# Moving the state-space constants of a two-block transformer kernel from VectorE to GpSimd

## The chip, the cores and the metric

The kernel runs on one core of a Trainium2 chip. A core has five engines that each work through a queue of their own, in order: TensorE (PE, matmuls; its weight loads are shown as PEld), VectorE (DVE), ScalarE (ACT), GpSimd (POOL) and SyncE (SP, which here issues the loads of the weights). An instruction waits at the head of its queue until the semaphores of its inputs allow it, and everything behind it on that engine waits too. The metric is device time in microseconds (us) for one execution, lower is better.

## The reference

The reference is a stack of two models on 256 tokens of width 1024. Only the first layer of the first model matters here. It projects the normalised input to a mix of an RWKV-7 recurrence (4 pairs of heads here) and a diagonal state-space model, S5, with 32 groups of 64 complex states. What the S5 part computes from its parameters, before any token is touched, is:

```
lam     = complex(lam_re, lam_im)
dt      = exp(log_dt)[:, None]
lam_bar = exp(lam * dt)
b_bar   = ((lam_bar - 1.0) / lam)[..., None] * complex(b_re, b_im)
bu      = einsum('gpi,btgi->btgp', b_bar, ug)
states  = scan(x_t = lam_bar * x_(t-1) + bu_t)
y       = real(einsum('gip,btgp->btgi', complex(c_re, c_im), states)) + d_skip * ug
```

followed by a gelu and a gate. The 32 x 64 states are laid out as 128 partitions x 16 columns, so that each step on the constants is one operation on a 128x16 tile.

## The kernel before, in words

The kernel goes through ten phases. The first, mix0, holds what the change touches. It normalises the input and transposes it (norm_T, L385 transposes, L361 xTh on ScalarE, L362 xTl on VectorE), and then projects it with weights that are split into a high and a low part: raw is loaded by SyncE into three buffers, ScalarE rounds it (L270, whi), VectorE subtracts (L271, wlo, 128x1024), and TensorE does three matmuls for each product (L320 to L322). The projections come in pairs of blocks (zpair), in the order WA, G0, k0, r0, v0, k1, ... Each block is scaled and token-shifted (L1060 to L1062, zs and z).

Between the normalisation and the RWKV code stands s5_prep, the function that is changed. It loads three tiles (s5l, s5b, s5c) from ScalarE's queue; computes two exponentials by range reduction and a polynomial of degree eight (exp_parts, names dt... and rho...); reduces the angle to (-pi, pi); has ScalarE take one Sine of 128x48 (L1388, tile sn, with a table load); renormalises the cosine and sine (unit, tiles m1 and m2); forms the factor wr + i wi of the B weights with one reciprocal (L1416); multiplies the B weights with it in six GpSimd operations of 128x512 (L1425 to L1427, tiles e2 and bt, shown as e and bt); lets TensorE transpose e2 (L1434) and ScalarE copy the result to WB (L1435); and last squares the cosine and sine seven times for the powers 2, 4, ..., 128 of the rotation (tiles qc and qs). All operations on 128x16 tiles but the Sine are VectorE's, most of them through the helper tt, whose line is L1359.

Who uses the results: WB and rho go into s5_main, whose first matmuls (L1480) come after all projections; the powers go into s5_table (L1453 to L1462), in which GpSimd doubles a table of cosines and sines seven times, from 128x16 to 128x1024. That table lies in memory that the transposed input xTh and xTl held, so it starts after the last projection's matmul.

GpSimd has other short work in the same stretch, in ew, once for each pair of heads: th (L1133), which VectorE's scan L1144 reads, and a (L1139); and zG (L1082). Each is a 128x256 operation between two of other engines.

The order of each engine's queue is not written out by hand in this stage. The kernel is built with a scheduler of the library (TileContext with schedule_with_timeline_sim=True), which plays the program against its own costs of the instructions and puts each instruction into its engine's queue in the order of that play; on the chip the queues keep that order. Semaphores are placed for each dependence, within an engine too. The functions of RWKV are generators that are stepped in turns (drive), which sets the order in which the scheduler meets them.

Of the kernel before, what the change touches and what calls it, by code (L numbers as in the profile page):

```python
# [204 lines left out]
def build(tc, dram, off, out, phases):  # L205
# [10 lines left out]
    V, S, G, T = nc.vector, nc.scalar, nc.gpsimd, nc.tensor  # L216
# [9 lines left out]
    def psC(shape=(128, 512)):  # L226
        return pp.tile(list(shape), F32, tag="C", name="psC", bufs=2)
# [747 lines left out]
    def mix0():  # L975
        nonlocal junk_at
        with tc.tile_pool(name="z", bufs=1, reuse_waits="tile") as zp:
# [16 lines left out]
            with tc.tile_pool(name="rw", bufs=1, reuse_waits="tile") as rp:  # L994
                open_kv(0)
                zx, s5x = ExitStack(), ExitStack()
                zxp = zx.enter_context(tc.tile_pool(name="zx", bufs=1, side="right", reuse_waits="tile"))
                junk_at = (zxp, 512)
                xh, xl, rm = norm_T(ht, "norm_mix0", xp=zxp)
                bcast_row(rm, zp, rrow)  # L1000
                with tc.tile_pool(name="s5prep", bufs=1, reuse_waits="tile") as sp:
                    s5c = s5_prep(zp, sp)

                def s5():
                    zx.close()
                    sp = s5x.enter_context(tc.tile_pool(name="s5", bufs=1, side="right", reuse_waits="tile"))
                    yield from s5_table(sp, s5c)
                    yield from s5_main(sp, s5c, yab, uT)

                rwkv(rp, zpair, yab, uT, rrow, s5())  # L1010
                s5x.close()
# [316 lines left out]
    def gb(x, n=32):  # L1328
        return x[:, :, None].to_broadcast([128, 16, n])

    def s5_prep(zp, sp):
        def t16(name, n=1):
            keep = name in ("rho", "sn") or name[0] == "q"
            return (zp if keep else sp).tile([128, n * 16], F32, name=name)

        lv = sp.tile([128, 48], F32, name="s5l")
        S.dma_start(lv, dram("s5l"))
        bb = sp.tile([128, 2, 512], F32, name="s5b")
        S.dma_start(bb.rearrange("p a b -> p (a b)"), dram("s5b"))
        cc = zp.tile([128, 2, 16, 32], F32, name="s5c")  # L1340
        S.dma_start(cc.rearrange("p a b c -> p (a b c)"), dram("s5c"))
        S.mul(cc[:, 1], cc[:, 1], -1.0)
        lr, li, ld = lv[:, :16], lv[:, 16:32], lv[:, 32:]

        def exp_parts(x, tag):
            n, r, q, s = [sp.tile([128, 16], F32, name=tag + c) for c in "nrqs"]
            V.tensor_scalar(x, x, -87.0, 87.0, op0=ALU.max, op1=ALU.min)
            V.tensor_scalar(n, x, 1.0 / math.log(2.0), 12582912.0, op0=ALU.mult, op1=ALU.add)
            V.tensor_scalar(n, n, -12582912.0, None, op0=ALU.add)
            V.scalar_tensor_tensor(r, n, -0.693359375, x, op0=ALU.mult, op1=ALU.add)  # L1350
            V.scalar_tensor_tensor(r, n, 2.12194440e-4, r, op0=ALU.mult, op1=ALU.add)
            V.tensor_scalar(q, r, 1.0 / 40320, None, op0=ALU.mult)
            for f in (5040, 720, 120, 24, 6, 2, 1):
                V.scalar_tensor_tensor(q, q, 1.0 / f, r, op0=ALU.add, op1=ALU.mult)
            V.tensor_scalar(s.bitcast(I32), n, 127.0, 8388608.0, op0=ALU.add, op1=ALU.mult)
            return q, s

        def tt(o, a, b, op):
            V.tensor_tensor(o, a, b, op=op)  # L1359
            return o  # L1360

        q, s = exp_parts(ld, "dt")
        dt = t16("dt")
        V.scalar_tensor_tensor(dt, q, 1.0, s, op0=ALU.add, op1=ALU.mult)
        ar, th = t16("ar"), t16("theta")
        tt(ar, lr, dt, ALU.mult)
        tt(th, li, dt, ALU.mult)
        q, s = exp_parts(ar, "rho")
        rho, rm1 = t16("rho"), t16("rm1")
        V.scalar_tensor_tensor(rho, q, 1.0, s, op0=ALU.add, op1=ALU.mult)  # L1370
        tt(rm1, q, s, ALU.mult)
        V.scalar_tensor_tensor(rm1, s, -1.0, rm1, op0=ALU.add, op1=ALU.add)
        n, an = t16("turns"), t16("ang", 3)
        r = an[:, :16]
        V.tensor_scalar(n, th, 1.0 / (2 * math.pi), 12582912.0, op0=ALU.mult, op1=ALU.add)
        V.tensor_scalar(n, n, -12582912.0, None, op0=ALU.add)
        c1 = 6.28125
        c2 = 2029.0 / 2 ** 20
        c3 = 2 * math.pi - c1 - c2
        V.scalar_tensor_tensor(r, n, -c1, th, op0=ALU.mult, op1=ALU.add)  # L1380
        V.scalar_tensor_tensor(r, n, -c2, r, op0=ALU.mult, op1=ALU.add)
        V.scalar_tensor_tensor(r, n, -c3, r, op0=ALU.mult, op1=ALU.add)
        V.tensor_scalar(r, r, 3.1415925, -3.1415925, op0=ALU.min, op1=ALU.max)
        V.scalar_tensor_tensor(an[:, 16:32], r, -1.0, r, op0=ALU.mult, op1=ALU.max)
        V.tensor_scalar(an[:, 16:32], an[:, 16:32], -1.0, math.pi / 2, op0=ALU.mult, op1=ALU.add)
        V.tensor_scalar(an[:, 32:], r, 0.5, None, op0=ALU.mult)
        sn = t16("sn", 3)
        S.activation(sn, an, AF.Sin)  # L1388
        m1, m2 = t16("m1"), t16("m2")

        def unit(c, s):
            tt(m1, c, c, ALU.mult)
            tt(m2, s, s, ALU.mult)
            tt(m1, m1, m2, ALU.add)
            V.tensor_scalar(m1, m1, -0.5, 1.5, op0=ALU.mult, op1=ALU.add)
            tt(c, c, m1, ALU.mult)
            tt(s, s, m1, ALU.mult)

        si, co, hs = sn[:, :16], sn[:, 16:32], sn[:, 32:]
        unit(co, si)  # L1400
        br, bi, w1, w2 = t16("br"), t16("bi"), t16("w1"), t16("w2")
        tt(hs, hs, hs, ALU.mult)
        tt(br, rm1, co, ALU.mult)
        V.scalar_tensor_tensor(br, hs, -2.0, br, op0=ALU.mult, op1=ALU.add)
        tt(bi, rho, si, ALU.mult)
        wr, wi = t16("wr"), t16("wi")
        tt(w1, br, lr, ALU.mult)
        tt(w2, bi, li, ALU.mult)
        tt(wr, w1, w2, ALU.add)
        tt(w1, bi, lr, ALU.mult)  # L1410
        tt(w2, br, li, ALU.mult)
        tt(wi, w1, w2, ALU.subtract)
        tt(w1, lr, lr, ALU.mult)
        tt(w2, li, li, ALU.mult)
        tt(w1, w1, w2, ALU.add)
        V.reciprocal(w2, w1)  # L1416
# [12 lines left out]
        for j2 in range(2):  # L1429
            pt = psC((128, 2, 2, 128))  # L1430
            for a in range(2):
                for i in range(2):
                    j = 2 * j2 + a
                    T.transpose(pt[:, a, i], e2[:, i, 4 * j:4 * j + 4].rearrange("p g i -> p (g i)"), ident)  # L1434
            S.copy(WB[:, 2 * j2:2 * j2 + 2], pt)  # L1435

        pw = [(co, si)]
        for i in range(7):
            pc, ps = pw[-1]
            qc, qs = t16("qc%d" % i), t16("qs%d" % i)  # L1440
            tt(m1, pc, pc, ALU.mult)
            tt(m2, ps, ps, ALU.mult)
            tt(qc, m1, m2, ALU.subtract)
            V.scalar_tensor_tensor(qs, pc, 2.0, ps, op0=ALU.mult, op1=ALU.mult)
            unit(qc, qs)
            pw.append((qc, qs))
        return {"pw": pw, "rho": rho, "WB": WB, "cc": cc}
# [384 lines left out]
```

## Time and profile before

| | |
|---|---|
| median of 3 runs | 2523.37 us (2523.07 to 2532.45) |
| the profiled execution | 2523.59 us, of it the span from the first to the last instruction 2521.7 us |
| instructions | 39316; PE 14335, DVE 3506, ACT 2268, POOL 145 |
| mean granted TensorE clock | 0.971 of full speed (2.4 GHz) |

The profile divides the span into stretches; the first phase, mix0, takes about the first 340 us of it. In a timeline each row has the start, the duration (or the sum of those of merged instructions), the engine, the line and the operation, what it writes and reads with the shapes, and in brackets how long the engine stood idle just before and what released it. Two neighbours on an engine may overlap in their rows, since an instruction starts before its forerunner's results have landed. A buffer's number is left out of a tile's name, so e1 and e2 both show as e.

### The profile page before, as it was taken

How to read it: one execution, taken by the hardware profiler on the slowest of the kernel's cores; microseconds unless marked ns; L12 is line 12 of the kernel's file. 1: busy time of each engine (PE TensorE's matmuls, PEld its weight loads, DVE VectorE, ACT ScalarE, POOL GpSimd, SP SyncE). 2: the span in 40 equal slices, each digit the busy share in tenths (PEclk: the TensorE clock that was granted, in tenths of full speed). 3: DMA queues.
4: the chain of work that ended last, by engine and by line, in shares of the span. 5: the costliest groups of instructions: out<-in, count | busy, mean ns of one | idle time of the engine just before them, and what ended most of it. 6: DMA issues, size and time to landing. Idle time of an engine off the chain costs nothing. (4 is left out here: it accounts for less than half of the span.)

```text
span 2521.7 us, 39316 instructions
## 1 busy us (share of the span) xinstructions
PE 2404.3 (95%) x14335; PEld 1997.5 (79%) x14335; DVE 2035.8 (81%) x3506; ACT 1515.2 (60%) x2268; POOL 115.7 (5%) x145
## 2 busy tenths in 40 slices
PE   7888979999999999999999999999998999999999
PEld 6765757999777778787878787877786789976998
DVE  8599665766776679999999999998987778877886
ACT  6322245544665567777777777777766555565554
POOL 2442200000000000000000000000000000000000
PEclk9988979999899989999999999999998999999999
DMA  5311134555444569999999999999994345552553
GB/s 181 109 35 34 52 113 138 190 185 177 154 134 142 192 212 372 345 333 356 362 346 334 357 360 331 359 325 365 348 363 148 118 160 190 186 176 96 182 186 108
DMA packets 154761, 558.19 MB, mean 221 GB/s; under 512 B 17568, under 2 KB 18208, under 8 KB 154560
## 3 DMA queue, kind: packets, MB, share of 16 engines
q1 hardware_dynamic: 152064, 551.62, 62.4%
q10 hardware_dynamic: 2496, 3.99, 0.5%
q8 instruction: 114, 1.87, 0.3%
q14 instruction: 87, 0.71, 0.1%
HBM read 554.50 MB, written 1.05 MB: 220 GB/s over the span
## 5 line engine op out<-in xcount | busy, mean ns | idle before, releaser
L271 DVE TENSOR_TENSOR wlo<-raw,whi 128x1024 fp32r<-128x1024 f32 x1044 | 1253.0, 1226 | 221.3 <-ACT whi L270 207.8
L270 ACT CAST whi<-raw 128x1024 fp32r<-128x1024 f32 x1044 | 1074.7, 1051 | 509.6 <-PE psA L322 213.0
L321 PE MATMUL psB<-wlo,xeh 128*128 128x512 f32 x880 | 351.4, 399 | 3.3 <-DVE wlo L271 3.3
L322 PE MATMUL psB<-whi,xel 128*128 128x512 f32 x880 | 347.6, 395 | 0.0
L320 PE MATMUL psB<-whi,xeh 128*128 128x512 f32 x880 | 345.8, 396 | 0.1
L321 PE MATMUL psB<-xTl,whi 128*128 128x256 f32 x1008 | 283.8, 282 | 0.0
L320 PE MATMUL psB<-xTh,whi 128*128 128x256 f32 x1008 | 281.5, 283 | 1.5 <-DVE fg L1743 1.5
L322 PE MATMUL psB<-xTh,wlo 128*128 128x256 f32 x1008 | 282.6, 281 | 0.0
L321 PEld LDWEIGHTS psB<-wlo,xeh 128*128 128x128 f32 x880 | 165.2, 188 | 47.6 <-DVE wlo L271 9.6
L320 PEld LDWEIGHTS psB<-whi,xeh 128*128 128x128 f32 x880 | 165.2, 188 | 40.0 <-ACT whi L270 1.0
L322 PEld LDWEIGHTS psB<-whi,xel 128*128 128x128 f32 x880 | 165.3, 188 | 38.1
L322 PEld LDWEIGHTS psB<-xTh,wlo 128*128 128x128 f32 x1008 | 191.0, 189 | 0.4
L320 PEld LDWEIGHTS psB<-xTh,whi 128*128 128x128 f32 x1008 | 187.8, 188 | 3.2 <-DVE fg L1743 2.1
L321 PEld LDWEIGHTS psB<-xTl,whi 128*128 128x128 f32 x1008 | 189.4, 188 | 1.1
L321 PE MATMUL psA<-wlo,mhh 128*128 128x512 f32 x448 | 175.8, 394 | 0.2
L320 PE MATMUL psA<-whi,xTh 128*128 128x512 f32 x416 | 170.6, 419 | 5.1 <-ACT whi L270 4.8
L322 PE MATMUL psA<-whi,mhl 128*128 128x512 f32 x448 | 173.8, 392 | 1.2 <-DVE mhl L359 1.2
L321 PE MATMUL psA<-wlo,xTh 128*128 128x512 f32 x416 | 168.7, 409 | 0.1
L322 PE MATMUL psA<-whi,xTl 128*128 128x512 f32 x416 | 163.9, 409 | 0.0
L320 PE MATMUL psA<-whi,mhh 128*128 128x512 f32 x448 | 152.4, 392 | 1.7 <-ACT mhh L358 1.7
L320 PE MATMUL psA<-whi,hh 128*128 128x512 f32 x264 | 103.4, 392 | 1.5 <-ACT hh L358 1.5
L321 PE MATMUL psA<-wlo,hh 128*128 128x512 f32 x264 | 103.2, 391 | 0.0
(568 smaller groups left out, 3901.7 us busy)
## 6 DMA issues: line engine op xcount, KB each, us to landing
raw<-in_w_moe SPq DMA_DIRECT2D x672, 512.0 KB, 6.0
raw<-in_w_bfu SPq DMA_DIRECT2D x88, 512.0 KB, 4.6
raw<-in_w_ffu SPq DMA_DIRECT2D x44, 512.0 KB, 4.5
raw<-in_w_bfd SPq DMA_DIRECT2D x44, 512.0 KB, 4.5
raw<-in_w_kv SPq DMA_DIRECT2D x32, 512.0 KB, 3.6
raw<-in_w_in SPq DMA_DIRECT2D x32, 512.0 KB, 5.7
raw<-in_w_qkv SPq DMA_DIRECT2D x24, 512.0 KB, 4.5
raw<-in_w_ffd SPq DMA_DIRECT2D x22, 512.0 KB, 4.4
```

What stands on the lines that cost most here:

```text
L270: S.copy(hi, raw[:, r])
L271: V.tensor_tensor(lo, raw[:, r], hi.bitcast(F32), op=ALU.subtract)
L320: T.matmul(ps, ah, bh, start=st, stop=False)
L321: T.matmul(ps, ah, bl, start=False, stop=False)
L322: T.matmul(ps, al, bh, start=False, stop=sp)
```

## The change

The helper tt and the plain tensor_scalar operations of s5_prep go to GpSimd (G) instead of VectorE (V). The operation scalar_tensor_tensor, out = (x op0 c) op1 y, becomes two GpSimd operations through one new tile sc of 128x16, in a helper stt. Five operations stay on VectorE: the clamp of each exponent (L1347), the clamp and the absolute value of the angle (L1383, L1384) and the reciprocal (L1416). The Sine stays on ScalarE, and nothing outside s5_prep is edited.

```diff
+        sc = sp.tile([128, 16], F32, name="sc")
+
+        def stt(o, x, c, y, op0, op1):
+            G.tensor_scalar(sc, x, c, None, op0=op0)
+            G.tensor_tensor(o, sc, y, op=op1)
+
...
             V.tensor_scalar(x, x, -87.0, 87.0, op0=ALU.max, op1=ALU.min)
-            V.tensor_scalar(n, x, 1.0 / math.log(2.0), 12582912.0, op0=ALU.mult, op1=ALU.add)
-            V.tensor_scalar(n, n, -12582912.0, None, op0=ALU.add)
-            V.scalar_tensor_tensor(r, n, -0.693359375, x, op0=ALU.mult, op1=ALU.add)
...
+            G.tensor_scalar(n, x, 1.0 / math.log(2.0), 12582912.0, op0=ALU.mult, op1=ALU.add)
+            G.tensor_scalar(n, n, -12582912.0, None, op0=ALU.add)
+            stt(r, n, -0.693359375, x, op0=ALU.mult, op1=ALU.add)
+            stt(r, n, 2.12194440e-4, r, op0=ALU.mult, op1=ALU.add)
+            G.tensor_scalar(q, r, 1.0 / 40320, None, op0=ALU.mult)
             for f in (5040, 720, 120, 24, 6, 2, 1):
-                V.scalar_tensor_tensor(q, q, 1.0 / f, r, op0=ALU.add, op1=ALU.mult)
-            V.tensor_scalar(s.bitcast(I32), n, 127.0, 8388608.0, op0=ALU.add, op1=ALU.mult)
+                stt(q, q, 1.0 / f, r, op0=ALU.add, op1=ALU.mult)
+            G.tensor_scalar(s.bitcast(I32), n, 127.0, 8388608.0, op0=ALU.add, op1=ALU.mult)
             return q, s
 
         def tt(o, a, b, op):
-            V.tensor_tensor(o, a, b, op=op)
+            G.tensor_tensor(o, a, b, op=op)
             return o
...
         V.tensor_scalar(r, r, 3.1415925, -3.1415925, op0=ALU.min, op1=ALU.max)
         V.scalar_tensor_tensor(an[:, 16:32], r, -1.0, r, op0=ALU.mult, op1=ALU.max)
-        V.tensor_scalar(an[:, 16:32], an[:, 16:32], -1.0, math.pi / 2, op0=ALU.mult, op1=ALU.add)
-        V.tensor_scalar(an[:, 32:], r, 0.5, None, op0=ALU.mult)
+        G.tensor_scalar(an[:, 16:32], an[:, 16:32], -1.0, math.pi / 2, op0=ALU.mult, op1=ALU.add)
+        G.tensor_scalar(an[:, 32:], r, 0.5, None, op0=ALU.mult)
...
-            V.tensor_scalar(m1, m1, -0.5, 1.5, op0=ALU.mult, op1=ALU.add)
+            G.tensor_scalar(m1, m1, -0.5, 1.5, op0=ALU.mult, op1=ALU.add)
...
-            V.scalar_tensor_tensor(qs, pc, 2.0, ps, op0=ALU.mult, op1=ALU.mult)
+            stt(qs, pc, 2.0, ps, op0=ALU.mult, op1=ALU.mult)
             unit(qc, qs)
```

The same exchange is made at the other scalar_tensor_tensor (dt, rho, rm1, the three steps of the angle's reduction, br) and at the two tensor_scalar of the angle's turns.

## Rows read from the trace of the kernel before

**Rows 1.** The page, busy time, share of the span and instructions of two engines.

```profile
PE 2404.3 (95%) x14335; PEld 1997.5 (79%) x14335; DVE 2035.8 (81%) x3506; ACT 1515.2 (60%) x2268; POOL 115.7 (5%) x145
```

**Rows 2.** Windows: stretch, its length, busy us (instructions), granted clock, DMA share, GB/s.

```profile
20.00:60.00 40.00, 34.24 (x261) 31.02 (x259) 38.30 (x159) 27.06 (x63) 11.73 (x11) 1.00 0.40 125
60.00:100.00 40.00, 39.40 (x443) 36.20 (x445) 32.97 (x87) 19.91 (x33) 2.39 (x8) 1.00 0.46 148
```

**Rows 3.** Timeline around zG and the third pair's th, four engines.

```profile
103.07 0.42 ACT L1081 ACTIVATE zG<-zG 128x256 f32<-128x256 f32 x1 [1.19 <-DVE zG L1062]
105.62 0.41 POOL L1082 TENSOR_SCALAR zG<-zG 128x256 f32<-128x256 f32 x1
111.42 0.49 ACT L1132 ACTIVATE th<-psB,hw 128x256 f32<-128x256 f32 x1
124.71 0.85 POOL L1133 TENSOR_SCALAR th<-th 128x256 f32<-128x256 f32 x1
125.60 0.87 DVE L1144 TENSOR_TENSOR_SCAN th<-rwc,th 128x256 f32<-128x256 f32 x1 [12.69 <-POOL th L1133]
127.89 0.48 PE L1238 MATMUL psC<-TZ,rwc 64*64 64x64 f32 x4 [9.93 <-ACT TZ L1243]
```

**Rows 4.** Timeline of VectorE, first clamp and two small operations of s5_prep.

```profile
6.46 0.17 DVE L1347 TENSOR_SCALAR s5l<-s5l 128x16 f32<-128x16 f32 x1 [0.98 <-DMA s5l<-in_s5l]
...
21.68 0.17 DVE L1359 TENSOR_TENSOR w<-bi,s5l 128x16 f32<-128x16 f32 x1
21.77 0.17 DVE L1359 TENSOR_TENSOR w<-br,s5l 128x16 f32<-128x16 f32 x1
```

**Rows 5.** Timeline of GpSimd, the first steps of the sine table.

```profile
99.34 0.13 POOL L1453 MEMSET ctab<- 128x16 f32 x1 [17.07 <-PE psA L322]
...
99.56 0.23 POOL L1460 TENSOR_TENSOR ctab<-ctab,sn 128x16 f32<-128x16 f32 x1
99.74 0.23 POOL L1460 TENSOR_TENSOR stab<-ctab,sn 128x16 f32<-128x16 f32 x1
99.93 0.28 POOL L1461 TENSOR_TENSOR u<-stab,sn 128x16 f32<-128x16 f32 x1
100.29 0.25 POOL L1462 TENSOR_TENSOR ctab<-ctab,u 128x16 f32<-128x16 f32 x1
100.62 0.28 POOL L1461 TENSOR_TENSOR u<-stab,sn 128x16 f32<-128x16 f32 x1
100.86 1.22 POOL L1460 TENSOR_TENSOR ctab<-ctab,qc 128x32 f32<-128x32 f32 x1
```

**Rows 6.** Timeline of VectorE, the wlo beside them.

```profile
100.74 1.24 DVE L271 TENSOR_TENSOR wlo<-raw,whi 128x1024 fp32r<-128x1024 f32 x1
```

**Rows 7.** Groups by form on VectorE, 6 to 60 us: count, busy us, mean ns.

```profile
L271 DVE TENSOR_TENSOR wlo<-raw,whi 128x1024 fp32r<-128x1024 f32 x11 | 15.4, 1398 | 0.8 <-ACT whi L270 0.7
```

**Rows 8.** Timeline: first and last of six multiplications, first th, first transposes.

```profile
27.84 1.05 POOL L1425 TENSOR_TENSOR e<-s5b,wr 128x512 f32<-128x512 f32 x1
...
34.69 1.30 POOL L1427 TENSOR_TENSOR e<-e,bt 128x512 f32<-128x512 f32 x1
36.46 1.33 POOL L1133 TENSOR_SCALAR th<-th 128x256 f32<-128x256 f32 x1 [0.47 <-ACT th L1132]
37.46 0.38 PE L1434 MATMUL psC<-ident,e 128*128 128x128 f32 x2
```

**Rows 9.** Timeline of ScalarE, the Sine.

```profile
13.63 1.28 ACT L1388 ACT_TABLE_LOAD   x1
14.93 0.24 ACT L1388 ACTIVATE sn<-ang 128x48 f32<-128x48 f32 x1
```

**Rows 10.** Windows, after TensorE's idle time; columns as in rows 2.

```profile
127.90:142.00 14.10, 10.76 (x164) 9.48 (x166) 13.65 (x26) 1.84 (x3) 8.64 (x5) 0.62 0.02 3
```

**Rows 11.** Timeline of TensorE at the start, last slow and a fast matmul.

```profile
18.00 0.41 PE L321 MATMUL psA<-xTl,whi 128*128 128x256 f32 x1
18.54 0.28 PE L320 MATMUL psA<-xTh,whi 128*128 128x256 f32 x1
```

More of the change, by code (lines that the diff above doesn't have):

```diff
@@ L1347, in exp_parts @@
             V.tensor_scalar(x, x, -87.0, 87.0, op0=ALU.max, op1=ALU.min)
-            V.tensor_scalar(n, x, 1.0 / math.log(2.0), 12582912.0, op0=ALU.mult, op1=ALU.add)
-            V.tensor_scalar(n, n, -12582912.0, None, op0=ALU.add)
-            V.scalar_tensor_tensor(r, n, -0.693359375, x, op0=ALU.mult, op1=ALU.add)
-            V.scalar_tensor_tensor(r, n, 2.12194440e-4, r, op0=ALU.mult, op1=ALU.add)
-            V.tensor_scalar(q, r, 1.0 / 40320, None, op0=ALU.mult)
+            G.tensor_scalar(n, x, 1.0 / math.log(2.0), 12582912.0, op0=ALU.mult, op1=ALU.add)
[3 more added lines that the diff above has]
+            G.tensor_scalar(q, r, 1.0 / 40320, None, op0=ALU.mult)
             for f in (5040, 720, 120, 24, 6, 2, 1):
-                V.scalar_tensor_tensor(q, q, 1.0 / f, r, op0=ALU.add, op1=ALU.mult)
-            V.tensor_scalar(s.bitcast(I32), n, 127.0, 8388608.0, op0=ALU.add, op1=ALU.mult)
+                stt(q, q, 1.0 / f, r, op0=ALU.add, op1=ALU.mult)
+            G.tensor_scalar(s.bitcast(I32), n, 127.0, 8388608.0, op0=ALU.add, op1=ALU.mult)
             return q, s
         def tt(o, a, b, op):
-            V.tensor_tensor(o, a, b, op=op)
+            G.tensor_tensor(o, a, b, op=op)
             return o
@@ L1363, in s5_prep @@
         dt = t16("dt")
-        V.scalar_tensor_tensor(dt, q, 1.0, s, op0=ALU.add, op1=ALU.mult)
+        stt(dt, q, 1.0, s, op0=ALU.add, op1=ALU.mult)
         ar, th = t16("ar"), t16("theta")
@@ L1369, in s5_prep @@
         rho, rm1 = t16("rho"), t16("rm1")
-        V.scalar_tensor_tensor(rho, q, 1.0, s, op0=ALU.add, op1=ALU.mult)
+        stt(rho, q, 1.0, s, op0=ALU.add, op1=ALU.mult)
         tt(rm1, q, s, ALU.mult)
-        V.scalar_tensor_tensor(rm1, s, -1.0, rm1, op0=ALU.add, op1=ALU.add)
+        stt(rm1, s, -1.0, rm1, op0=ALU.add, op1=ALU.add)
         n, an = t16("turns"), t16("ang", 3)
         r = an[:, :16]
-        V.tensor_scalar(n, th, 1.0 / (2 * math.pi), 12582912.0, op0=ALU.mult, op1=ALU.add)
-        V.tensor_scalar(n, n, -12582912.0, None, op0=ALU.add)
+        G.tensor_scalar(n, th, 1.0 / (2 * math.pi), 12582912.0, op0=ALU.mult, op1=ALU.add)
+        G.tensor_scalar(n, n, -12582912.0, None, op0=ALU.add)
         c1 = 6.28125
@@ L1379, in s5_prep @@
         c3 = 2 * math.pi - c1 - c2
-        V.scalar_tensor_tensor(r, n, -c1, th, op0=ALU.mult, op1=ALU.add)
-        V.scalar_tensor_tensor(r, n, -c2, r, op0=ALU.mult, op1=ALU.add)
-        V.scalar_tensor_tensor(r, n, -c3, r, op0=ALU.mult, op1=ALU.add)
+        stt(r, n, -c1, th, op0=ALU.mult, op1=ALU.add)
+        stt(r, n, -c2, r, op0=ALU.mult, op1=ALU.add)
+        stt(r, n, -c3, r, op0=ALU.mult, op1=ALU.add)
         V.tensor_scalar(r, r, 3.1415925, -3.1415925, op0=ALU.min, op1=ALU.max)
         V.scalar_tensor_tensor(an[:, 16:32], r, -1.0, r, op0=ALU.mult, op1=ALU.max)
-        V.tensor_scalar(an[:, 16:32], an[:, 16:32], -1.0, math.pi / 2, op0=ALU.mult, op1=ALU.add)
-        V.tensor_scalar(an[:, 32:], r, 0.5, None, op0=ALU.mult)
+        G.tensor_scalar(an[:, 16:32], an[:, 16:32], -1.0, math.pi / 2, op0=ALU.mult, op1=ALU.add)
+        G.tensor_scalar(an[:, 32:], r, 0.5, None, op0=ALU.mult)
         sn = t16("sn", 3)
@@ L1403, in s5_prep @@
         tt(br, rm1, co, ALU.mult)
-        V.scalar_tensor_tensor(br, hs, -2.0, br, op0=ALU.mult, op1=ALU.add)
+        stt(br, hs, -2.0, br, op0=ALU.mult, op1=ALU.add)
         tt(bi, rho, si, ALU.mult)
```

## The prediction

> **What bounds the kernel now.** I read the busy shares first: TensorE is busy 95% of the span and VectorE 81% [rows 1]. That is an average over very different stages, so the table by stretch comes next, for the stage in which the moved operations run. They are VectorE operations that begin with the first clamp at 6.46 us [rows 4] and run among the first projections. From 20 to 60 us VectorE is busy 38.30 of 40 us and TensorE 34.24; from 60 to 100 us TensorE is busy 39.40 of 40 and VectorE 32.97 [rows 2]. So up to about 60 us VectorE sets the pace, and afterwards the matmuls do. TensorE's idle time from 20 to 60 us, 40 - 34.24 = 5.8 us, is about all that a lighter VectorE can give back there; after 60 us there is 0.6 us left to win.
>
> The third view is the GpSimd queue against those that wait for it. In the same stage there is already one place where small work behind other GpSimd work stops everything: th (L1133) of the third head pair. Its input, ScalarE's L1132, ends at 111.42 + 0.49 = 111.91 us, but GpSimd is inside the sine table and reaches th at 124.71. VectorE stands 12.69 us at the scan L1144 that needs it, and TensorE then stands 9.93 us [rows 3]. The reader should keep two things of this: the queues run in the order that was fixed when the program was built, and that order had counted on GpSimd being further on.
>
> **The change, part by part.**
>
> *Off VectorE.* Counting s5_prep line by line: 13 operations move in each of the two exponentials (26), 10 in each of seven powers (70), 34 elsewhere: 130. Five stay on VectorE: two clamps of the exponents, the clamp and absolute value of the angle, the reciprocal. Neighbours that need not wait start 0.09 us apart (21.68, 21.77) though each lasts 0.17 [rows 4], so the relief is about 130 x 0.09 = 11.7 us of VectorE's time. As TensorE takes over as the bound, I count it at the 5.8 us of idle time above, rounded to 6 us.
>
> *Onto GpSimd.* 32 of the 130 were scalar_tensor_tensor and become two operations each through the one tile sc: 130 + 32 = 162 instructions, 85 before the B weights and 77 in the powers. The trace has no such chain on GpSimd, but the first steps of the sine table have the shape. Two 128x16 operations that do not depend on each other start 0.18 us apart (99.56, 99.74); a dependent one starts 0.36 or 0.33 us after its producer (99.93, 100.29, 100.62) [rows 5]. A 128x16 TENSOR_SCALAR is not shown on GpSimd; it lies between the 128x16 MEMSET of 0.13 and the TENSOR_TENSOR of 0.23 to 0.28, and I price it as the latter since its wait for the producer is the same. All independent gives 162 x 0.18 = 29 us, all dependent 162 x 0.36 = 58. The exponentials and all 64 instructions through sc are dependent; about 45 of the 162 (second squares, second products) have a neighbour that need not wait. I take 117 x 0.33 + 45 x 0.18 = 46.7 us, 0.29 each.
>
> *The two engines get in each other's way.* The 128x32 operation at 100.86 took 1.22 us, those of 128x16 before it 0.23 to 0.28: VectorE's wlo ran from 100.74 to 101.98 [rows 5, 6]. So a two-input operation of GpSimd waits for such a one of VectorE. Eleven wlo run from 6 to 60 us [rows 7]: between 0 and 11 x 1.2 = 13 us are added to GpSimd's chain, and I take 1 us for each of the four or so before the B weights.
>
> *When the B weights are ready.* Before their multiplications come 85 instructions, and about 20 of the powers, independent of them, slip into gaps: 105 x 0.29 = 30 us. Sine needs a table load of 1.28 and 0.24 us on ScalarE [rows 9], and there are three short trips to VectorE: 2 us. With 4 us for wlo: 36 us after the first clamp at 6.5, so 43 us. The six multiplications took 27.84 to 35.99 = 8.2 us [rows 8] and still do: 51 us, 15 us later than now. TensorE's transposes of e (L1434) now start at 37.46, 1.5 us after the last of them [rows 8].
>
> *Who waits.* Transposes stand in TensorE's fixed order; behind them are the rest of the projections. th (L1133) of the first head pair stands in GpSimd's queue at 36.46, now with an idle engine ahead of it [rows 8]; behind VectorE's scan of it are the wlo of all later weights. Sine stands in ScalarE's queue; behind it are the xTh and whi of the first weights, on which TensorE's first projection waits. If the order were built with true GpSimd times, other work would be put in front of each and nothing would stand. The trace says how far off it is: zG (L1082) was ready at 103.07 + 0.42 = 103.49, 3.9 us after the table's first multiplication at 99.56, and ran 6.1 us after; th was ready 12.4 us after and ran 25.2 after [rows 3, 5]. If each was put in the queue for the moment at which its input came, GpSimd takes 1.5 times the counted time over small operations and 2 times over the whole table. Ends for small ones: 1.0 (zG's delay was the one wlo, its 0.98 us, and chance) to 2.0. I take 1.5, the row nearest in size. Then the 44 us to the end of e were counted as 44 / 1.5 = 29, and TensorE reaches the transposes some 15 us too early. The waits of sine, the clamps, the reciprocal and th are the same lag met earlier or on another queue, not more of it: the largest counts.
>
> *Restart.* After its 9.9 us idle TensorE ran at a granted clock of 0.62 from 127.9 to 142 us, a mix of the two levels, the lower for most of it [rows 10]. At the start of the kernel it was the same for 4.6 us: matmuls of 0.41 us until 18.2, 0.28 from 18.54 [rows 11]. That costs 4.6 x (1 - 0.28 / 0.41) = 1.5 us at least, and up to 14 x 0.4 = 5.6 us.
>
> *Nothing else moves.* The three loads (s5l, s5b, s5c) stay where they are, GpSimd issues no DMA, and SyncE's weight loads follow the buffers that the casts free. Chain, e and the waiting th, a, zG end at 6.5 + 46.7 + 2 + 11 + 8.2 + 4 = 78 us; the sine table multiplies from 99.56 on [rows 5], when the last projection frees its memory, so the 21 us between are cover for it. Even at 0.36 each, 90 us, the table would not start later by this chain.
>
> *Sum.* -6 (relief) + 15 (lag) + 1.5 (restart) = +10.5 us; as some of the lag falls in TensorE's idle time that is already counted, +10. The profiled execution took 2523.59 us, of which the span is 2521.7, and the median of the runs is 2523.37: 2523.4 + 10 = 2533 us.
>
> *A rule against these rows.* GPSIMD is about 2x slower than VectorE on two-input elementwise work, says the Trainium skill, GPSIMD Engine Reference, section Engine selection. The rows show a larger factor at 128x16, 0.29 per instruction against 0.09, and 1.25 times as many of them. By the rule alone the chain would be an estimated 130 x 0.09 x 2 = 23 us and the transposes would wait for nothing, which is the first rival below; the measured starts decide for me.
>
> **Rivals.**
>
> 1. *GpSimd keeps up; faster.* Place: the transposes at 37.46. If the counted time for 128x16 operations is right (factor 1.0), other work stands in front of each wait, and only the relief is left: 2523.4 - 6 = 2517 us; the full 11.7 us off VectorE would be 2512. It decides from the point where the lag is under 6 us, a factor below 44 / 38 = 1.16. For it: zG's small delay, of which one wlo is half. Against it: th's 12.8 us behind the same queue. Chance 0.17.
>
> 2. *The lag is larger and the restarts add up.* Price 0.36 per instruction, all wlo in the way, factor 2: e ends at 6.5 + 38 + 2 + 8 + 8.2 = 63 us, counted at 35: +28 - 6 + 4 = +26; the middle between that and the forecast, +18, gives 2541 us. For it: each of the five operations left on VectorE is a new trip between two engines, with wlo queued behind. Against it: while VectorE stands, nothing blocks GpSimd. Chance 0.15.
>
> 3. *The order shifts and an old wait goes.* The whole order is worked out anew, and th of the third pair may land ahead of the table: its 12.7 us go, 2533 - 12 = 2521 us. For it: that wait exists by a narrow margin of the order. Against it: the table still starts when the last projection frees its memory, so its order against th has no reason to change. Chance 0.08.
>
> **How the numbers follow.** The forecast has 0.60. A change of 0.5% is 12.6 us, about what a measurement can tell from none. The forecast (+10, from +2 to +18) has about 0.21 of its 0.60 beyond +12.6 and 0.39 within; rival 2 has 0.13 beyond; rival 1 has 0.03 below -12.6 and 0.14 within; rival 3 has 0.05 below (if it comes with rival 1) and 0.03 within. The remaining 0.02 of rival 2 is within. Faster 0.08, same 0.58, slower 0.34. For 8 in 10 the range runs from a little below rival 1 (2516) to between the two ends of rival 2 (2547); the forecast's own range is 2525 to 2541.
>
> **What would show it.** Right: GpSimd has 145 + 162 = 307 instructions, VectorE 3376; TensorE waits 8 us or more at L1434 for e, or VectorE as long at L1144 or a clamp for GpSimd; TensorE's busy time from 20 to 60 us falls below 34 us. Relief right: the wlo of the first 35 us come closer together. Wrong: the transposes wait less than 6 us; small GpSimd operations start under 0.22 us apart on average; or the last projection ends before 99 us.

## The result, and the profile after

The changed kernel is slower: 2548.84 us, the median of five runs (2540.74 to 2557.43), against 2524.49 us for the kernel before (2523.07 to 2532.45); the ratio is 1.009, with a 95% interval from 1.0075 to 1.0105. A second measurement gave 2547.65 us and 1.0088 (1.0071 to 1.0105). The forecast was 2533, with a range up to 2547. The profiled execution took 2540.74 us, with a span of 2539.0. Two executions further below, one of *powers only* (3350.55 us) and one of *and th on VectorE* (2714.45 us), ran at a far lower clock throughout, and the medians given there are without them.

The page's busy shares, to be held against [rows 1]:

```profile
PE 2408.0 (95%) x14335; PEld 1999.1 (79%) x14335; DVE 2024.2 (80%) x3376; ACT 1514.5 (60%) x2268; POOL 161.4 (6%) x307
```

The instruction counts are the forecast ones: 130 fewer on VectorE, 162 more on GpSimd. The windows that answer to [rows 2]:

```profile
20.00:60.00 40.00, 32.74 (x218) 30.17 (x218) 21.50 (x47) 25.58 (x58) 35.49 (x99) 0.87 0.32 101
60.00:100.00 40.00, 38.12 (x364) 34.51 (x363) 35.67 (x111) 18.88 (x33) 14.41 (x42) 1.00 0.47 151
```

From 20 to 60 us VectorE's busy time (third pair of columns) fell from 38.30 to 21.50 us, but TensorE did 218 matmuls instead of 261, and its granted clock fell from 1.00 to 0.87. To find where the time went, I cut the trace at two events that every kernel has: the first instruction of the sine table (it waits for the last projection's matmul) and the first update of h, which ends the first phase. First the kernel before, then the kernel after, in the columns of [rows 2]:

```profile
0.00:99.30 99.30, 82.95 (x736) 75.19 (x737) 83.93 (x333) 58.84 (x124) 14.49 (x24) 1.00 0.51 168
99.30:362.50 263.20, 220.39 (x2689) 164.80 (x2689) 191.14 (x449) 74.81 (x146) 87.24 (x95) 0.88 0.15 47
```

```profile
0.00:106.30 106.30, 86.91 (x734) 79.07 (x735) 70.87 (x204) 59.05 (x124) 61.12 (x186) 0.95 0.48 157
106.30:377.20 270.90, 222.70 (x2691) 164.17 (x2690) 192.67 (x449) 74.46 (x146) 86.84 (x95) 0.87 0.15 48
```

TensorE does the same matmuls in each part (736 and 734; 2689 and 2691), so the rows split a loss into two kinds: idle time (length less busy) and slower matmuls (busy). Up to the table the change loses 7.0 us: idle 106.30 - 86.91 = 19.39 against 16.35 us, +3.0, and busy +4.0. From the table to the update it loses 270.9 - 263.2 = 7.7 us: idle +5.4, busy +2.3. The rest of the program, 2161.8 against 2159.2 us, adds 2.6. That is the whole difference of the two spans, 2539.0 - 2521.7 = 17.3 us. The medians differ by 24.4 us; the 7 us more are taken up in the part on the prediction.

**The first part** is two stalls of TensorE, both begun by a wait for GpSimd. The timeline of the kernel after (start, duration; in brackets the idle time before and its releaser):

```profile
8.15 0.22 POOL L1340 TENSOR_TENSOR dtr<-sc,s5l 128x16 f32<-128x16 f32 x1
8.46 0.25 POOL L1339 TENSOR_SCALAR sc<-dtn 128x16 f32<-128x16 f32 x1
8.80 0.22 POOL L1340 TENSOR_TENSOR dtr<-sc,dtr 128x16 f32<-128x16 f32 x1
...
29.69 0.17 DVE L1389 TENSOR_SCALAR ang<-ang 128x16 f32<-128x16 f32 x1 [4.05 <-POOL ang L1340]
29.77 0.48 DVE L1062 SCALAR_TENSOR_TENSOR zWA<-zs,cols,zWA 128x255 f32<-128x255 f32 x1
30.29 0.42 ACT L1079 ACTIVATE zWA<-zWA 64x256 f32<-64x256 f32 x1 [5.29 <-DVE zWA L1062]
31.12 1.28 ACT L1394 ACT_TABLE_LOAD   x1
32.56 1.03 ACT L270 CAST whi<-raw 128x1024 fp32r<-128x1024 f32 x1
33.64 0.39 PE L320 MATMUL psA<-xTh,whi 128*128 128x256 f32 x1 [2.18 <-ACT whi L270]
...
38.30 0.21 POOL L1365 TENSOR_TENSOR m<-qc 128x16 f32<-128x16 f32 x1
38.48 0.22 POOL L1365 TENSOR_TENSOR wr<-w,w 128x16 f32<-128x16 f32 x1
...
41.01 1.23 POOL L1365 TENSOR_TENSOR wr<-wr,w 128x16 f32<-128x16 f32 x1
...
52.22 1.26 POOL L1433 TENSOR_TENSOR e<-e,bt 128x512 f32<-128x512 f32 x1
53.54 1.54 PE L1440 MATMUL psC<-ident,e 128*128 128x128 f32 x6 [2.49 <-POOL e L1433]
```

Read it as a relay. VectorE stands 4.05 us at the clamp of the angle (in [rows 4] it waited only for its own work); zWA is queued behind that clamp, ScalarE's tanh of zWA behind zWA, whi behind the tanh, and TensorE behind whi. Between the tanh and whi stand Sine's table load (31.12, 1.28 us) and Sine itself (32.41, 0.24), which in the kernel before ran as the first projections began [rows 9]; they waited for nothing, but they are 1.5 us of the 2.18 that TensorE stood. (The kernel before had another load of this length ahead of that tanh, at 25.26, but TensorE then had matmuls to do.) The second stall is the one that the prediction named, the transposes, but 2.49 us of it and not 15. A third wait, 3.35 us of VectorE at the reciprocal (40.50), did not hold TensorE up. Behind each stall the clock fell; windows of the two stretches:

```profile
35.60:39.00 3.40, 3.40 (x19) 3.40 (x18) 1.55 (x2) 0.51 (x1) 3.40 (x13) 0.50 0.66 230
52.70:59.50 6.80, 5.96 (x28) 5.97 (x29) 4.55 (x16) 5.36 (x15) 6.47 (x20) 0.50 0.27 77
```

A granted clock of 0.50 is the lower level, 1.2 GHz; (3.40 + 5.96) / 2 = 4.7 us is the price of matmuls at half speed, of which the sums above show 4.0 as longer busy time.

**The second part.** The old stall at th, in the pair that the prediction calls the third (it is the last of four), is still there (11.88 us; 12.69 in [rows 3]), and the table starts at 106.31 (99.34 in [rows 5]); then the order differs:

```profile
106.31 0.13 POOL L1459 MEMSET ctab<- 128x16 f32 x1 [16.94 <-PE psA L322]
...
132.46 2.38 DVE L1144 TENSOR_TENSOR_SCAN th<-rwc,th 128x256 f32<-128x256 f32 x1 [11.88 <-POOL th L1133]
...
142.53 0.68 DVE L1492 TENSOR_TENSOR M<-psA,ctab 128x512 f32<-128x512 f32 x1
...
154.44 0.41 DVE L1227 TENSOR_TENSOR Y<-psC,rwc 128x256 f32<-128x256 f32 x1
154.90 0.48 PE L1238 MATMUL psC<-TZ,rwc 64*64 64x64 f32 x4 [6.42 <-DVE Y L1227]
```

The kernel before has Y right behind the first M:

```profile
137.20 0.68 DVE L1486 TENSOR_TENSOR M<-psA,ctab 128x512 f32<-128x512 f32 x1
...
138.19 0.75 DVE L1227 TENSOR_TENSOR Y<-psC,rwc 128x256 f32<-128x256 f32 x2
```

After the change VectorE does most of the first block of the scan phase before that Y, and TensorE waits 6.42 us. No edited line lies here.

### The profile page after: what moved, and what is told of

The parts are those of the page before. It is cut to its first block, busy times and chain, and to the rows that moved or that the text cites. A ratio compares the mean times of both kernels' runs of the same rounds, so it can differ in the third digit from the quotient of the medians.

```text
span 2539.0 us, 39346 instructions
## 1 busy us (share of the span) xinstructions
PE 2408.0 (95%) x14335; PEld 1999.1 (79%) x14335; DVE 2024.2 (80%) x3376; ACT 1514.5 (60%) x2268; POOL 161.4 (6%) x307
```

## The experiments

The table holds what the text below reads: the start of the sine table; how much more TensorE was idle and busy before it than in the kernel before; the length from the table to the first update of h; the ratio to the kernel before with its interval. The times are from one profile of each, cut as above.

| kernel | table at | idle, busy | to update | ratio |
|---|---|---|---|---|
| before | 99.3 | | 263.2 | |
| after | 106.3 | +3.0, +4.0 | 270.9 | 1.009 (1.0075 to 1.0105) |
| no constants | 99.6 | 0.0, +0.3 | 260.5 | 1.000 (0.999 to 1.001) |
| powers only | 100.8 | -0.1, +1.6 | 264.0 | 1.0001 (0.9988 to 1.0014) |
| front only | 115.6 | +7.2, +9.1 | 289.4 | 1.0169 (1.0148 to 1.0191) |
| dead chain | 107.2 | +3.8, +4.1 | 263.3 | 1.003 (1.0016 to 1.0045) |
| no trips | 110.5 | +4.7, +6.5 | 265.7 | 1.0045 (1.0025 to 1.0064) |
| before, th on VectorE | 102.3 | +1.8, +1.2 | 261.8 | 1.0036 (1.0024 to 1.0049) |
| after, th on VectorE | 108.7 | +3.2, +6.2 | 279.8 | 1.009 (1.0073 to 1.0107) |
| after, one Y first | 105.4 | +1.8, +4.3 | 280.2 | 1.0081 (1.0067 to 1.0095) |
| four waits back | 103.8 | +2.6, +1.9 | 268.4 | 1.0059 (1.0046 to 1.0073) |
| five waits back | 101.3 | +1.1, +0.9 | 263.9 | 1.0041 (1.0027 to 1.0054) |
| and th on VectorE | 98.3 | -2.0, +1.0 | 272.2 | 1.0055 (1.0037 to 1.0072) |
| and a on VectorE | 99.4 | -0.1, +0.2 | 269.6 | 1.0049 (1.0035 to 1.0063) |
| before, other order | 99.4 | -0.1, +0.2 | 277.5 | 1.0094 (1.0073 to 1.0114) |

**The kernel after again**, for the repeat.

> The changed kernel once more, to see which of its losses repeat. In its first profile the sine table's first instruction (ctab) stood 7.0 us later than before (106.3 against 99.3) and the first update of h, the end of the first phase, 14.7 us later (377.2 against 362.5). Theory L (GpSimd reaches the end of a fixed chain late and in-order queues wait for it: VectorE 4.1 us at the angle's clamp, 3.4 at the reciprocal, TensorE 2.7 at e): the table starts at 106 within 1 us again. Rival T (TensorE's clock at its lower level in later phases makes the loss): these two anchors differ by more than 3 us from the first profile. Under both the total is 2540 to 2558, and what differs between two profiles of it lies behind the first phase.

2547.65 us; the table came at 105.8 and the update 270.7 us later, so both parts of the loss repeat.

**No constants.** What could be won at most:

```diff
-        q, s = exp_parts(ld, "dt")
...
+        G.memset(rho, 0.5)
+        G.memset(sn, 0.5)
+        G.memset(wr, 0.5)
+        G.memset(wi, 0.5)
...
+        pw = [(co, si)] * 8
```

> The constants are left out altogether: the tiles rho, sn, wr and wi are filled with a number by GpSimd, and the powers are the cosine and sine themselves. This measures the relief, which the prediction took as 6 us. If VectorE's moved operations are worth 6 us of the first stage, the table starts at 92 to 94 us; if it starts at 97 us or later, there was little to win whichever engine does them. The total follows the end of the first phase; the order behind the table may move it by up to 10 us either way.

2525.89 us. With no constants to compute (so its output has no meaning) the table starts where it did:

```profile
0.00:99.60 99.60, 83.21 (x737) 75.76 (x738) 72.78 (x199) 56.38 (x121) 13.60 (x29) 1.00 0.52 168
```

VectorE has 11.2 us less to do (83.93 to 72.78), and TensorE's idle time is the same 16.4 us. The relief is worth nothing in the sum, but not because none came. The start of both kernels, first that of before:

```profile
10.31 0.15 DVE L412 TENSOR_TENSOR ss<-ss 128x2 f32<-128x2 f32 x1
13.62 0.56 PE L320 MATMUL psA<-xTh,whi 128*128 128x256 f32 x1
```

```profile
9.58 1.05 POOL L1359 TENSOR_TENSOR bt<-s5b,wi 128x512 f32<-128x512 f32 x1
9.85 0.80 DVE L412 TENSOR_TENSOR ss<-ss 128x2 f32<-128x2 f32 x1 [0.26 <-ACT junk L401]
16.44 0.56 PE L320 MATMUL psA<-xTh,whi 128*128 128x256 f32 x1
```

```profile
20.00:60.00 40.00, 37.19 (x279) 34.33 (x278) 28.70 (x84) 27.07 (x65) 3.49 (x5) 1.00 0.46 140
```

Without the chain the multiplications of the B weights run on GpSimd from 8.58 us on, and beside them five of VectorE's operations of 128x2 in the normalisation took 0.80 to 1.11 us each instead of 0.15 to 0.17. The first projection starts 2.8 us late (16.44 against 13.62), and from there to the table the kernel needs 2.6 us less than before (83.1 against 85.7). In the window of the prediction, 20 to 60 us, TensorE's idle time fell from 5.8 to 2.8 us. So the relief was about 3 us, half of what was forecast, and this run lost as much ahead of it; it does not bound what a better order could win.

**Parts of the change.** Only the powers on GpSimd (an edit of the kernel before, below), and the converse, the kernel after with the powers on VectorE again:

```diff
-            tt(m1, pc, pc, ALU.mult)
+            G.tensor_tensor(g1, pc, pc, op=ALU.mult)
...
-            V.scalar_tensor_tensor(qs, pc, 2.0, ps, op0=ALU.mult, op1=ALU.mult)
+            G.tensor_scalar(sc, pc, 2.0, None, op0=ALU.mult)
+            G.tensor_tensor(qs, sc, ps, op=ALU.mult)
```

> Only the seven powers (77 instructions) run on GpSimd, the part before the B weights stays on VectorE as before. Theory L: nobody waits for the powers before the table, so the waits at clamp, reciprocal and e are gone and VectorE is 6 us lighter; the table starts at 95 to 99 us, time 2512 to 2526. Rival C (the two engines block each other by sharing their way to memory, whoever waits): 77 of 162 instructions give about half of the 7 us, the table starts at 101 to 104.

> Only the part before the B weights (85 instructions) runs on GpSimd, the powers stay on VectorE. Theory L: all three waits stay, the table starts at 104 to 108 us. Rival C: about half of the 7 us, 102 to 104. Total 2535 to 2560.

2527.73 and 2568.69 us. The 77 instructions of the powers, for which nobody waits before the table, cost nothing that can be measured in the whole, but the table came at 100.8 and not at the expected 95 to 99: TensorE waited 1.7 us for e. The 85 before the B weights cost more alone than the whole change. The rows of the second show four stalls of TensorE of 1.8 to 2.9 us before the table, and another order behind it (289.4); why so much more than after was not tried.

**A dead chain** in the kernel before, ahead of all else on GpSimd:

```diff
+        for _ in range(81):
+            G.tensor_scalar(z1, lr, 0.5, None, op0=ALU.mult)
+            G.tensor_tensor(z2, z1, li, op=ALU.mult)
```

> The kernel before, with 162 more instructions of 128x16 on GpSimd whose results nobody reads (a TENSOR_SCALAR and a TENSOR_TENSOR by turns, each waiting for the one before). Theory L: only th, a, e and zG can stand behind them; the table starts at 99 to 103 us. Rival C: the blocking alone gives the 7 us, 105 to 107.

2532.45 us. Nobody reads the chain, yet the table is 7.9 us late (107.2), not within the expected 99 to 103 but where the rival had it that the two engines block each other. The rows show a wait in a queue, for the multiplications of the B weights stand behind the chain:

```profile
40.09 1.26 POOL L1431 TENSOR_TENSOR e<-e,bt 128x512 f32<-128x512 f32 x1
41.40 0.69 PE L1438 MATMUL psC<-ident,e 128*128 128x128 f32 x2 [5.34 <-POOL e L1431]
```

```profile
0.00:107.20 107.20, 87.02 (x737) 79.48 (x738) 82.30 (x334) 59.11 (x124) 69.94 (x187) 0.95 0.48 156
40.10:50.40 10.30, 9.00 (x38) 8.12 (x39) 4.64 (x15) 5.03 (x14) 9.53 (x20) 0.50 0.18 49
```

One stall of 5.34 us, then 10.3 us at half clock. VectorE's busy time is not longer than before (82.30 against 83.93), so this load of GpSimd does not slow VectorE here. And behind the table, where VectorE's order came out as in the kernel before (the same through the end of the phase and far beyond), the length is that of before, 263.3.

**No trips to VectorE.** Clamps on GpSimd, the absolute value replaced by a comparison on GpSimd (not shown), the reciprocal computed early:

```diff
-            V.tensor_scalar(x, x, -87.0, 87.0, op0=ALU.max, op1=ALU.min)
+            G.tensor_scalar(x, x, -87.0, 87.0, op0=ALU.max, op1=ALU.min)
...
+        V.reciprocal(i2, il)
+        q, s = exp_parts(ld, "dt")
```

> The changed kernel without its trips between GpSimd and VectorE: clamps and the folding of the angle (a comparison in place of the absolute value) on GpSimd too, and the reciprocal taken at the start from tiles of its own, on VectorE, before any GpSimd result. Theory L: the waits of 4.1 and 3.4 us on VectorE are gone, TensorE's wait for e stays and may grow to 5; the table starts at 100 to 103 us. Rival C: 105 to 107, as in the changed kernel.

2535.75 us. The table came at 110.5, later than both theories had it. The waits did not go but moved: Sine now stood 5.90 us in ScalarE's queue, with zWA behind it, and TensorE 4.13 us. Behind the table the order was again that of before, and the length 265.7.

**th and a on VectorE**, in both kernels:

```diff
-            G.tensor_scalar(th, th, 1.0, None, op0=ALU.add)
+            V.tensor_scalar(th, th, 1.0, None, op0=ALU.add)
```

> The kernel before, with th (L1133) and a (L1139) on VectorE in place of GpSimd. The third pair's th then doesn't stand behind the table: VectorE's 12.7 us and TensorE's 9.9 us are gone, at a price of 8 x 0.3 us of VectorE. If that stall is on the path: 2509 to 2516 us. If other work waits for the table in its place: 2520 to 2528.

> The changed kernel with th and a on VectorE. Theory: of the 14.7 us that the first phase lost, 7 come from the chain and 7.7 from the third pair's th and the order around it. Then this kernel is only about 7 us slower than the kernel before with th and a on VectorE. Rival O (the second part is the new order by itself, with or without the wait): 12 us or more slower than that.

2533.78 and 2549.04 us. In the kernel before the last scan came 9.4 us earlier (116.2 against 125.6), and the phase ended 1.6 us later: a Y of VectorE then held TensorE for 10.7 us. Taking the largest old stall away won nothing; both expected ranges ended at 2528 or below. The two kernels differ by 15.3 us, more than the 12 that spoke for the rival of the second, a new order that costs with or without the old wait.

**One Y first**, in the kernel after:

```diff
+                    yield from idle(1)
...
+                    with tc.issue_after(held["Y"]) if gp == 0 else nullcontext():
+                        V.tensor_tensor(M, pb, cb, op=ALU.mult)
```

> The kernel after, with one order held: VectorE's first multiplication of the scan phase (L1492, M of the first of its 16 blocks) is queued behind a Y (L1227), and the phase's first block is met one step later; every queue of VectorE is the same as in the kernel after up to that M. Theory 'the second part of the loss is an order': from the start of the sine table to the first update of h the kernel after took 270.9 us and the kernel before 263.2, and the two experiments in which VectorE's order behind the fourth scan L1144 was the same as before took 265.7 and 263.3 though GpSimd had as much or more to do; so here 263 to 267 us, the table still at 106 us, and a profiled time 4 to 8 us under that of the kernel after (2532 to 2537 us against 2540); median 4 to 9 us under 2548. Rival 'the stretch is longer because the table is late or GpSimd is in the way': 270 to 272 us again, and the same time as after.

2545.7 us. The stretch became longer, 280.2. In it TensorE's waits for Y at these matmuls fell from 8.9 us to 0.8, but its waits for the scan phase's own R grew from 11.2 to 25.1: that putting this one Y first wins the time back, as I read the stall of 6.42 us, is refuted.

**The order of after in the kernel before:**

```diff
+            with tc.issue_after(held["M"]) if p == 3 and "M" in held else nullcontext():
+                V.tensor_scalar(n2, pn.rearrange("p a b -> p (a b)"), 1e-24, None, op0=ALU.max)
...
+                with tc.issue_after(held["M2"]) if "M2" in held and held.setdefault("n", 0) < 1 else nullcontext():
+                    V.tensor_tensor(Y, pY, lmb(j + 1), op=ALU.mult)
```

> The kernel before, its constants on VectorE, with the order that the kernel after has behind the fourth scan L1144: VectorE's n2 (L1150) of the last head pair is queued behind the scan phase's first M (L1486), and the first of the two Y (L1227) behind the second M of the first block (L1513), which puts the whole first block ahead of both Y, as in the kernel after; up to there every queue is that of the kernel before. Theory 'the second part of the loss is the order that the scheduler chose behind the fourth scan, and has nothing to do with GpSimd': table at 99.3 us as before, 268 to 274 us from there to the first update of h (before 263.2, after 270.9), and 5 to 11 us over the kernel before. Rival 'the order is worth nothing, the stretch is longer because TensorE's clock or GpSimd's table came later': 262 to 265 us and the time of the kernel before within 2 us. That holding the one Y first in the kernel after made the stretch longer and not shorter speaks for this rival, or for another part of the order.

2547.96 us, as slow as the changed kernel, with the constants on VectorE and the front as before:

```profile
0.00:99.40 99.40, 83.14 (x737) 75.33 (x738) 83.95 (x334) 58.85 (x124) 14.52 (x25) 1.00 0.51 168
99.40:376.90 277.50, 227.09 (x2688) 167.04 (x2688) 192.15 (x449) 74.68 (x146) 86.59 (x95) 0.85 0.14 45
```

```profile
149.81 0.74 DVE L1232 TENSOR_TENSOR Y<-psC,rwc 128x256 f32<-128x256 f32 x2
150.37 0.48 PE L1245 MATMUL psC<-TZ,rwc 64*64 64x64 f32 x4 [9.40 <-DVE Y L1232]
```

TensorE stood 9.40 us at that Y. An order alone is worth 14.3 us in this stretch: up to the fourth scan every operation of VectorE behind the table stands as in the kernel before, and from there on they are nearly in after's order (the first 21 the same).

**The waits moved back.** The kernel after with every wait for the chain queued later; the work stays on GpSimd. First the clamp, Sine, the reciprocal and the transposes:

```diff
+        with tc.issue_after(held["V"]):
+            V.tensor_scalar(r, r, 3.1415925, -3.1415925, op0=ALU.min, op1=ALU.max)
...
+        with tc.issue_after(held["S"]):
+            S.activation(sn, an, AF.Sin)
```

> The kernel after, with the four places at which another engine waits for the chain moved back in their queues: the clamp and the absolute value of the angle behind VectorE's zs of block r0, Sine behind ScalarE's operation on the same block, the reciprocal behind zs of r1, TensorE's transposes of e behind the matmuls of block u1. GpSimd does all of the 162 instructions, as in the kernel after. Theory 'only the place of the waits costs': no idle gap of TensorE over 1.5 us between 25 and 100 us but the one of 1.9 us that the kernel before has at 35, no stretch at half clock before the table, the table at 99 to 102 us (after: 106.3; before: 99.3); its order behind the fourth scan is nearly that of before, so 262 to 267 us from there to the first update of h, and a median of 2523 to 2530 us (ratio 0.999 to 1.002). Rival 'GpSimd's load itself slows the stage (VectorE and GpSimd in each other's way)': the table at 105 us or later, as with the dead chain (107.2), and a median above 2531.

2541.43 us, table at 103.8, between the ranges of the two theories. The first scan came at 38.3 (before 41.1), and TensorE had no stall over 0.4 us and no half clock between 25 and 52 us; then it stood 2.96 us, again through GpSimd: th of the second pair stood behind e. So e went behind th, and the transposes behind block u3:

```diff
+            with tc.issue_after(held["G"]):
+                G.tensor_tensor(e2[:, i], b3[:, 0], gb(x), op=ALU.mult)
```

> The experiment with the waits moved back, with the one that was left: GpSimd's first multiplication of the B weights (e) is queued behind th (L1133) of the second head pair, which in that experiment stood behind four of them, so that VectorE's scan, ScalarE's D and whi and TensorE (3.0 us at 52 us) waited; the transposes move behind the matmuls of block u3. All 162 instructions stay on GpSimd. Theory 'only the places of the waits cost, and the 130 operations taken off VectorE are worth 2 to 3 us': no gap of TensorE over 1.5 us between 25 and 80 us but for one like that of before at 35, no half clock before the table, the table at 96 to 99.5 us (before 99.3). Rival 'nothing is won, the matmuls bound the stage whatever is taken off VectorE': 99.5 to 102. Rival 'GpSimd's load slows the stage': 103 or later. From the table to the first update of h 262 to 270 us, by the order that comes out; median 2522 to 2532.

2535.72 us, table at 101.3, as the rival had it by which nothing is won. The last one left, th behind the powers:

```profile
50.43 0.85 POOL L1140 TENSOR_SCALAR th<-th 128x256 f32<-128x256 f32 x1
51.32 1.52 DVE L1151 TENSOR_TENSOR_SCAN th<-rwc,th 128x256 f32<-128x256 f32 x1 [3.28 <-POOL th L1140]
54.83 0.39 PE L325 MATMUL psA<-xTh,wlo 128*128 128x256 f32 x1 [3.19 <-DVE wlo L274]
```

So th, and then a too, went to VectorE, with the diff of the experiment on th above:

> The experiment with five waits moved back, and with th (L1133) on VectorE, so that VectorE's scan of it no longer stands behind GpSimd's small operations; nothing but a, zG, the chain and e is left on GpSimd, and nothing that another engine needs soon stands behind the chain but a. In that experiment th of the second pair stood 5.1 us behind powers, the scan 3.3 us, TensorE 3.2 us at 51.6 us, and the table came at 101.3. Theory 'only the places of the waits cost, and the operations taken off VectorE are worth 2 to 3 us': no gap of TensorE over 1.5 us between 25 and 80 us, no half clock before the table, the table at 95.5 to 98.5 us (before 99.3). Rival 'the matmuls bound the stage, nothing is won': 99 to 101. Rival 'GpSimd's load slows the stage': 101.3 again or later. From the table to the first update of h 260 to 275 us by the order that comes out; the total follows that, 2520 to 2538.

> As the one with th on VectorE, and a (L1139) on VectorE as well. The front should be the same within 1 us (table 95.5 to 98.5 by the theory that only the places of the waits cost; 99 to 101 if nothing is won). What is told apart is the rest: the order of VectorE's queue behind the fourth scan comes out otherwise once more (both Y and the M between them ahead of the first block). Theory 'order': the stretch from the table to the first update of h differs by 3 us or more between the two, although GpSimd, the table and the front are the same. Rival: within 2 us of each other.

2538.27 and 2536.67 us. In the first the table comes 1.0 us earlier than in the kernel before, in the second 0.1 later, all 162 instructions being on GpSimd:

```profile
0.00:98.30 98.30, 83.94 (x738) 77.06 (x739) 74.88 (x206) 59.05 (x125) 63.10 (x183) 0.98 0.51 170
98.30:370.50 272.20, 226.04 (x2687) 165.91 (x2687) 191.12 (x449) 73.78 (x145) 84.75 (x94) 0.86 0.15 48
```

The +7.0 became 4.5, 2.0 and then -1.0: the first part was the places of the waits (the last step took th off GpSimd as well). The relief shows here too: from 20 to 60 us TensorE was busy 37.19 us, as without the constants; around and behind 60 us, stalls (of up to 1.33 us in the first) and a short stretch at a lower clock took most of it back in the first and all of it in the second. The two differ by 2.6 us behind the table, which is less than the 3 us I had set and more than the rival's 2, so the pair decides nothing; both lose 6 to 9 us there. The orders that are neither that of before nor of after give from 260.5 to 289.4 us in the table. None of these versions beats the kernel before; that none could, under another order, is not shown.

**The kernel after, for its profile:**

> The kernel after once more, for its profile alone: both profiles so far fell on the fastest of its runs (2540.7 and 2539.8 us, half of the clock granted for 160 and 157 us), while its median is 2548. If the profile falls on a run of 2546 us or more, it shows in which phase the rest goes: theory 'half clock in the later phases': the same first 377 us, and some 15 us more at half clock behind them. Rival: the first phase itself is longer (over 385 us).

2542.07 us (table 105.4, first update 378.8), not the 2546 that the question needed; it got no answer.

## Why the prediction was wrong

*Nothing else moves* is the step that failed. I had counted loads, DMAs and memory, and took the order of work behind the table as given. The 7.7 us there are nearly half of the profiled difference. With the same load on GpSimd and the order of before, down to the last operation of VectorE in this stretch, the loss is 0.1 and 2.5 us (dead chain 263.3, no trips 265.7), and an order like after's, put into the kernel before, costs 14.3 us. So the load alone does not do it and an order can; which detail of after's order is open, since holding the one Y made it worse.

The order moved far behind the phase too. From the update of h (L484) that starts at 2228.0 us in the kernel before to the one at 2322.3, seven of the 17 profiles have the order of before on TensorE and VectorE and take 92.5 to 94.4 us; the ten with another order, the three of the changed kernel among them, take 97.4 to 98.4. How late a kernel arrives there does not part them: the seven are 0 to 45 us behind the kernel before at that point, the ten from 2.8 us ahead to 22 behind. In the profiled execution of the changed kernel this stretch costs 3.8 us, more than the 2.6 of everything behind the first phase.

*The profiled execution and the median.* I took them as equal, as they were for before. The changed kernel's median is 8.1 us above its profiled execution, and its three profiled executions (2540.74, 2539.79, 2542.07) lie below all seven others (2546.46 to 2557.43). Without these 8 us the time would have been inside the range. The granted clock of the median run is 0.966 against 0.969: 0.003 less on the mean is 0.006 x 2547 = 15 us more at the lower level, at half speed some 7.6 us, an estimate from rounded means that is about the difference. In which stretch, and why, no profile shows; this part of the loss stays open.

*Relief, -6 us.* Too large: of TensorE's 5.8 idle us in [rows 2], 2.8 stay without the constants and with the waits moved back, so some 3 us were VectorE's load. At the table nothing of it was left without the constants (the late first projection) and 1.0 or -0.1 us with the waits moved back. I had counted all idle time of the window as VectorE's, and nothing against it.

*The chain, 46.7 us.* Met in the sum: GpSimd's busy time up to the table grew by 61.12 - 14.49 = 46.6 us. Its make-up is another. Dependent neighbours start 0.31 to 0.34 us apart (8.15, 8.46, 8.80), independent ones 0.18 (38.30, 38.48), as priced, but 12 of the 162 took 0.9 us or more, like the 1.23 at 41.01, and hold 14.5 us of the sum; the prediction had such waits on top, so the other 150 cost less than its 0.29 each (0.21 us of busy time). The estimate by the rule of the Trainium skill (GPSIMD Engine Reference, section Engine selection) was half of it, 23 us; the measurement decides against it at this size.

*e done at 51, chain at 78.* 53.5 and 73.0. The cover of 21 us up to the table was there.

*The lag of 15 us.* The direction was right (TensorE waits for e, and VectorE at a clamp), the size wrong, and the prediction's own sign of being wrong (the transposes wait less than 6 us) came true: 2.5 us at the transposes, since they were now queued at 50.4 and not at 37.5 us. The factor of 1.5, taken from zG, did not hold: the last of e landed 3.1 us after the first transpose (53.5 against 50.4), so the order had GpSimd's pace nearly right. And I had written that only the largest of the waits counts; two counted, one behind the other.

*Restart, 1.5 us.* 4.0, within the bound of 5.6 that I gave. In the dead chain it cost 4.1 for one stall. The reading of [rows 11] was wrong: those rows overlap, the slow matmuls start 0.21 us apart and the fast ones 0.12, so by the starts the 4.6 us cost 2.0; and the granted clock of that stretch reads 1.00, so it does not show the lower level. Relief, lag and restart, -6 + 15 + 1.5, were in truth +3.0 idle, which holds the relief, and +4.0; that my sum at the table, +10, came near to +7.0 is luck, by errors that cancel.

*Rivals.* GpSimd keeping up: nearly so for the pace, yet no gain followed. The larger lag gave 2541 us, the time of the profiled execution, by a mechanism that did not happen. That the whole order is worked out anew stood in the third rival, but there as a gain; the old wait at th stayed, and removing it in the kernel before won nothing.

## What to carry to other kernels

A busy engine is only in part a late one: before moving work off an engine, leave that work out and time the kernel, and look in its trace at what else moved. Here that run took the same time as before, 2.6 us won among the projections and 2.8 lost ahead of them, and so said in advance that there was little to win. When queues are in a fixed order, ask of a moved chain what stands behind each wait for it, on every engine, and move those waits back before judging the move. And any edit that makes a scheduler order the work anew can shift a stretch that it does not touch by as much as the edit itself is worth (7.7 against 7.0 us here), and others 2000 us later as well (3.8).

## What was not expected of the hardware

Some short stalls of TensorE cost about twice their length in this stage: 2.18 us idle was followed by 3.4 us at 1.2 GHz, 2.49 us by 6.8, 5.34 us by 10.3, and half of such a stretch is lost. It is no rule: 1.90 us idle at 37.12 in the kernel before was followed by a granted clock of 1.00. In the table the largest losses have both parts (+3.0, +4.0; +4.7, +6.5; +7.2, +9.1), but *powers only* lost 1.6 us of busy time with no more idle time than before.

Without the constants five of VectorE's 128x2 operations took 0.80 to 1.11 us beside GpSimd's of 128x512 (0.15 to 0.17 in the kernel before), and in the changed kernel 12 small operations of GpSimd took 0.9 us or more, while VectorE was no slower beside the 162 small ones of the dead chain (82.30 us busy against 83.93).
